# Attention values kept undivided, their divisors sent through DRAM to the output projection

## The chip, the core and the metric

The kernel runs on one core of one Trainium2 chip. A core has five engines with an instruction queue each: PE (matmuls), DVE (vector operations), ACT (activations and copies), POOL and SP (here only the issuing of DMAs). Sixteen DMA engines move data between DRAM and the core's memory, SBUF; matmul results stand in a small memory of their own, PSUM. The metric is device time in microseconds (us) for one execution of the whole program; "before" is 4280.88 us, the median of three runs (4253.56 to 4290.66).

## What is computed

One inference step of a two-layer decoder (D_MODEL 1024) for two groups at once: 1024 prompt positions and 8 sequences of 8 sample positions. Layer 0 mixes with an RWKV-7 recurrence, layer 1 with attention over 256 keys that an indexer selects; each is followed by a feed-forward network (FFN). The part that the change touches is layer 1's prompt attention and its output projection:

```python
def sparse_attend(q, kg, vg, valid):
    ...
    s = jnp.einsum('bthgd,btshd->bthgs', qg, kg.astype(F32)) * ATT_HEAD_DIM ** -0.5
    s = jnp.where(valid[:, :, None, None, :], s, -jnp.inf)
    p = jax.nn.softmax(s, axis=-1)
    o = jnp.einsum('bthgs,btshd->bthgd', p, vg.astype(F32))
    return o.reshape(B, T, Q_W).astype(q.dtype)
...
            o = attn_fn(j, q, k, v, qi, ki, wi) @ P['att_w_o'][j]
...
        x = x + g_a * o
        h = rms_norm(x, P['norm_g'][i, 1]) * (1 + sc_f) + sh_f
        u = jax.nn.relu(h @ P['w_up'][i])
        x = x + g_f * ((u * u) @ P['w_down'][i])
```

There are 16 query heads of 64 values, 4 to each of 4 key heads. The division by the softmax's sum is linear in each head's output, so it can be made at any point before the projection sums over heads.

## The kernel before

The work is split into two groups: A holds the 64 sample positions and prompt positions 0 to 511 (576 columns), B prompt positions 512 to 1023 (512 columns). Activations stand transposed, features on partitions and positions along the free axis, in eight chunks of 128 features. Matmuls in full precision are made of three: a high part `hi` and a rest `lo` of the activation against a high part `wh` and a rest `wl` of the weight (`mm3`, L140). `loadw` brings 128x1024 weights in (L120, SP), ACT casts the high part (L122), DVE or POOL makes the rest (L126). `split` does the same for activations: ACT the `hi` (L144), DVE the `lo` (L145).

The prompt attention runs tile by tile, 128 positions at a time, four tiles in each group. `att_post` (before it) normalizes and rotates queries and keys and computes the indexer's scores `sc` (L1164, L1166), `topk` finds each row's threshold on DVE (L1204). In `att_tile`, `scores(h)` makes one head's exponentials `sm` and their sums and takes the inverse `rs` (L1277), and `values(h)` takes two heads: it transposes `sm` on PE (`pt`, L1293), copies it (`PT`, L1295), multiplies with the values into one half of a PSUM tile `po` (L1299), and spreads the two inverses over 64 partitions with two more matmuls against the identity into `po`'s other half (L1304). After every second call, for the four heads of one key head, ACT copies the inverses out (`orb`, L1308), DVE multiplies (`oT`, L1310), and a DMA stores the tile to a DRAM buffer, `OA` or `OB` (L1311).

`out_proj` starts with eight loads `yl` from that buffer (L445, one for each chunk of 128 features, that is two heads), splits each into `hi` and `lo`, and then makes eight output chunks; each starts with the first chunk's `hi` and needs all eight. `resid` adds the result to the residual stream on DVE (L397). The FFN follows: `up` (matmuls, ACT's `z` at L416 and L417, `split` into `uh` and `ul`) and `down`. The `yl` tiles come from a pool that also serves the FFN's temporaries: 9 buffers, in the last output projection a pool of 6.

The code is written as generators: A's output projection and FFN are a side stream that advances while B's attention is written, and a list scheduler that goes by estimated durations then puts every engine's instructions in one fixed order, in which they run. So A's FFN matmuls stand between B's attention matmuls on PE, and an instruction that waits holds all that stands behind it on its engine. SP issues nearly every DMA of the program in one order as well. A's `out_proj` is entered at about 2990 us, while B's first tiles are in `att_post`; B's is entered at about 3642 us, when its last tile is done, with some of A's FFN still ahead of it on PE.

Of the kernel before, what the change touches and what calls it, by code (L numbers as in the profile page):

```python
# [15 lines left out]
ALU = mybir.AluOpType  # L16
# [3 lines left out]
D = 1024  # L20
# [57 lines left out]
class Kern:  # L78
# [357 lines left out]
            self.fbs = fb  # L436
            yield "fb"

    def out_proj(self, g, l, W_, src, x):

        nc, W = self.nc, g.W
        hi, lo = self.new_hl()
        for k in range(8):
            t = self.tmp("yl")
            nc.sync.dma_start(t[:, 0:W], src[k, :, 0:W])  # L445
            self.split(t[:, 0:W], self.ch(hi, k, W), self.ch(lo, k, W))
        xs = [(self.ch(hi, k, W), self.ch(lo, k, W)) for k in range(8)]
        for m in range(8):
            h, lw = self.loadw(W_[:, m * 128:m * 128 + 128].rearrange("(k p) f -> p k f", p=128), 128, 1024)
            self.mm3(g, [(h[:, k * 128:k * 128 + 128], lw[:, k * 128:k * 128 + 128]) for k in range(8)], xs, self.resid(g, l, 2, x, m))  # L450
            yield
# [791 lines left out]
    def att_tile(self, g, i, pp, bias, Lm):  # L1243


        nc = self.nc
        c0, n, kind, r0 = g.tiles[i]
        j = r0 // 128
        L = r0 + 128
        T1 = lambda nm, shape, dt=F32, tag=None, bufs=None: pp.tile(shape, dt, name=nm, tag=tag or nm, bufs=bufs)  # L1250
        nb = (L + 511) // 512
        nsm, npt, nq = (4, 3, 1) if Lm > 512 else (3, 2, 1)
        q = {}
        sms = {}
        out = {}

        def scores(h):
            gk, hh = divmod(h, 4)
            if hh == 0:
                qn = T1("qnl", [128, 4, 2, 64], bufs=nq)  # L1260
                for b in range(2):
                    nc.sync.dma_start(qn[:, :, b, :], self.scr["P" + g.name][i, :, gk * 256:gk * 256 + 256].rearrange("t (h d) -> t h d", d=64))
                q[gk] = self.att_q(pp, lambda h: qn[:, h].rearrange("p b d -> p (b d)"))
            qh, ql = q[gk]
            sm = T1("sm", [128, Lm], bufs=nsm)
            st = T1("st", [128, 4], bufs=6)
            mn, sums, rs = st[:, 0:2], st[:, 2:3], st[:, 3:4]
            for b in range(nb):
                k0, kn = b * 512, min(512, L - b * 512)
                ps = self.pss.tile([128, 512], F32, name="sp", tag="s")  # L1270
                self.att_qk(ps[:, 0:kn], qh, ql, hh, gk, k0, kn)
                nc.vector.tensor_tensor_reduce(out=sm[:, k0:k0 + kn], in0=ps[:, 0:kn], in1=bias[:, k0:k0 + kn], scale=-0.125, scalar=3.0e38,
                                               op0=ALU.add, op1=ALU.min, accum_out=mn[:, b:b + 1])
            if nb > 1:
                nc.vector.tensor_tensor(out=mn[:, 0:1], in0=mn[:, 0:1], in1=mn[:, 1:2], op=ALU.min)  # L1275
            nc.scalar.activation(out=sm[:, 0:L], in_=sm[:, 0:L], func=AF.Exp, scale=-1.0, bias=mn[:, 0:1], accum_out=sums)  # L1276
            nc.vector.reciprocal(out=rs, in_=sums)  # L1277
            sms[h] = sm, rs

        def values(h):  # L1280

            gk, hh = divmod(h, 4)
            if hh == 0:
                out[gk] = self.psy.tile([128, 512], F32, name="po", tag="y")
            pr = slice(hh // 2 * 128, hh // 2 * 128 + 128)
            half = lambda p: slice(p * 64, p * 64 + 64)
            for j0 in range(0, j + 1, 4):
                jn = min(4, j + 1 - j0)
                PTs = []
                for p in range(2):  # L1290
                    ps = self.lps("pt")
                    for jj in range(jn):
                        nc.tensor.transpose(ps[:, jj * 128:jj * 128 + 128], sms[h + p][0][:, (j0 + jj) * 128:(j0 + jj) * 128 + 128], self.ident)  # L1293
                    PT = T1("PT", [128, 512], bufs=npt)
                    (nc.scalar.copy if p else nc.vector.tensor_copy)(PT[:, 0:jn * 128], ps[:, 0:jn * 128])  # L1295
                    PTs.append(PT)
                for jj in range(jn):
                    for p in range(2):
                        nc.tensor.matmul(out[gk][half(p), pr], self.V[:, j0 + jj, gk * 64:gk * 64 + 64], PTs[p][:, jj * 128:jj * 128 + 128],  # L1299
                                         start=(j0 + jj == 0), stop=(j0 + jj == j))  # L1300

            for p in range(2):
                rs = sms.pop(h + p)[1]
                nc.tensor.matmul(out[gk][half(p), 256 + hh // 2 * 128:384 + hh // 2 * 128], rs.to_broadcast([128, 64]), self.ident, start=True, stop=True)  # L1304
            if hh == 2:
                po = out.pop(gk)
                rb = T1("orb", [128, 256])
                nc.scalar.copy(rb, po[:, 256:512])  # L1308
                oT = T1("oT", [128, 2, 128], bufs=2)
                nc.vector.tensor_tensor(out=oT, in0=po[:, 0:256].rearrange("p (a t) -> p a t", a=2), in1=rb.rearrange("p (a t) -> p a t", a=2), op=ALU.mult)  # L1310
                nc.sync.dma_start(self.scr["O" + g.name][gk * 2:gk * 2 + 2, :, c0:c0 + 128].rearrange("k p t -> p k t"), oT)  # L1311

        scores(0)
        scores(1)
        for h in range(0, 16, 2):
            if h < 14:
                scores(h + 2)
                scores(h + 3)
            values(h)
            yield  # L1320

    side = iter(())
    due = 0.0
# [21 lines left out]

    def att_prompt(self, g):
        self.scratch("O" + g.name, [8, 128, 576])
        with ExitStack() as ctx:
            P = lambda n, b, c=ctx, **k: c.enter_context(self.tc.tile_pool(name=n, bufs=b, **k))
            scp = P("asc", 1)  # L1350
            tk = P("atk", 1)
            S = [scp.tile([128, 640 + 128 * i], F32, name="sc%d" % i) for i in range(4)]
            with ExitStack() as c2:
                pp = P("attg", 1, c2)
                self.psl = P("psl4", 4, c2, space=PSUM)
                post = [self.att_post(g, i, pp, S[i]) for i in range(4)]
                self.together(RATES["post0B"], post[0:2])
                self.together(RATES["post2B"], post[2:4], [self.topk(tk, S[0:2])])
            pp = P("attt", 1)
            self.pss = P("pss", 2, space=PSUM)  # L1360
            self.psl = P("psl1", 1, space=PSUM)
            self.psy = P("psy", 1, space=PSUM)
            tiles = [self.att_tile(g, i, pp, S[i], 1024) for i in range(4)]
            self.together(RATES["tile0B"], tiles[0:2], [self.topk(tk, S[2:4])])
            self.together(RATES["tile2B"], tiles[2:4])

    def att_mixed(self):

        nc, I, g = self.nc, self.I, GA
        LS = PAST + 8  # L1370
        self.scratch("OA", [8, 128, 576])
        with ExitStack() as ctx:
            P = lambda n, b, c=ctx, **k: c.enter_context(self.tc.tile_pool(name=n, bufs=b, **k))
            pp = self.ap2 = P("atts", 1)
# [175 lines left out]
    def run(self):  # L1550
# [42 lines left out]
        self.ada_fin(0, 1)  # L1593
        self.ada_fin(1, 0)
        self.ada_fin(1, 1)
        def mixer(g, l, w, src, x):
            self.mark("out_proj" + g.name)
            yield from self.out_proj(g, l, w, src, x)
            self.mark("ffn" + g.name)
            yield from self.ffn(g, l, x)  # L1600

# [21 lines left out]

        def second(g):
            x = self.reload_x(g)
            yield from mixer(g, 1, self.I["att_w_o"][0], self.scr["O" + g.name], x)
            self.mark("store_y" + g.name)
            self.store_y(g, x)

# [15 lines left out]
        with ExitStack() as ctx:  # L1645
            self.mark("out_projB")
            x = self.xtile("xr", ctx.enter_context(self.tc.tile_pool(name="xp2", bufs=4)))
            old = self.act, self.up_
            self.act, self.up_ = [ctx.enter_context(self.tc.tile_pool(name=n, bufs=b)) for n, b in (("act3", 8), ("up3", 6))]
            x = self.reload_x(GB, x)  # L1650
            run(self.out_proj(GB, 1, self.I["att_w_o"][0], self.scr["OB"], x))
            hl = self.norm_hl(GB, 1, 1, x)
            self.act, self.up_ = old
            self.mark("ffnA")
            run(self.side)
            self.mark("ffnB")
            run(self.ffn(GB, 1, x, hl=hl))
            self.mark("store_yB")
            self.store_y(GB, x)
# [86 lines left out]
```

## Time and profile before

| | |
|---|---|
| time, median of 3 runs | 4280.88 us (4253.56 to 4290.66) |
| the profiled execution: time, span | 4286.67 us, 4284.8 us |
| mean granted TensorE clock | 0.915 |
| busy: PE, DVE, ACT, POOL | 3983.1, 2277.6, 1688.9, 964.0 us |
| A's attention tiles (two halves) | 2172 to 2330, 2330 to 2430 us |
| A's output projection entered | 2990 us |
| B's attention tiles (two halves) | 3272 to 3460, 3460 to 3640 us |
| B's output projection entered | 3642 us |

How to read the rows of the trace: the timeline gives start, duration, engine, line, operation, and output<-inputs, with the idle time of the engine ahead of the instruction and what ended it in brackets; equal neighbours are merged (x8). Line numbers are those of the kernel before. "SPq" is the queue from which DMAs are issued; the duration there is that of issuing, not of the transfer. A window's row gives its length, then for PE, weight loads, DVE, ACT and POOL the busy time and (instructions), then the granted clock as a share of full speed, the mean busy share of the 16 DMA engines and GB/s. A DMA view of a window counts packets, the pieces of a transfer, with their sizes.

### The profile page before, as it was taken

What the parts mean: (1) busy time and instruction counts of PE and PEld (TensorE: products, weight loads), DVE (VectorE), ACT (ScalarE), POOL (GpSimd) and SP (SyncE); (2) the same over time, 40 slices, a digit from 0 to 9 for tenths busy, and PEclk for the clock granted to TensorE, in tenths of its full rate; (3) what the DMA queues carried; (4) which work ended last, traced back from release to release, by engine and by line L of the source; (5) the groups of instructions that cost most, each with busy time, mean ns of one, the idle gap of its engine ahead of it and who ended that gap; (6) DMA issues with size and microseconds to landing.
All of it is one profiled execution on the core that took longest, in us unless ns stands there. A gap on an engine that the chain in (4) does not pass through costs nothing.

```text
span 4284.8 us, 76620 instructions
## 1 busy us (share of the span) xinstructions
PE 3983.1 (93%) x31120; PEld 3196.4 (75%) x31120; DVE 2277.6 (53%) x5534; ACT 1688.9 (39%) x3147; POOL 964.0 (22%) x762
## 2 busy tenths in 40 slices
PE   7998899998999999989799888989988999999999
PEld 5787665666777799989655555778767777988777
DVE  5512775543667533341886954332899854444232
ACT  5632554433445333331454333332443334324332
POOL 1321321311433222212111122222101000222222
PEclk6798787978999999999799999998879999999999
DMA  6676122323322122234332156335211111323332
GB/s 217 203 235 210 51 71 71 95 56 99 111 60 61 46 76 81 83 111 123 118 95 65 50 177 209 120 122 152 91 41 46 45 40 45 118 89 96 94 94 84
DMA packets 555889, 433.84 MB, mean 101 GB/s; under 512 B 93777, under 2 KB 517313, under 8 KB 550354
## 3 DMA queue, kind: packets, MB, share of 16 engines
q1 hardware_dynamic: 549650, 391.20, 30.5%
q0 software_dynamic: 5888, 37.75, 2.5%
q8 instruction: 245, 4.01, 0.4%
q14 instruction: 106, 0.87, 0.1%
HBM read 360.48 MB, written 67.87 MB: 100 GB/s over the span
## 4 chain that ended last, share of the span: by engine, by line
PE 70%; DVE 14%; issue 6%; ACT 3%; DMA 3%; POOL 1%; SPq 0%; DVEq 0%; ACTq 0%; POOLq 0%
PE o L140 42%; DVE tj L1204 3%; PE o L1035 3%; PE po L1299 2%; PE pt L1293 2%; PE sp L1186 1%; PE gp L706 1%; PE tp L733 1%; DMA kvraw<-in_cache_k,ix 1%; PE sp L1185 1%; PE rb L659 1%; POOL wl L126 1%; PE sps L1509 1%; PE tp L754 1%; PE spn L930 1%
## 5 line engine op out<-in xcount | busy, mean ns | idle before, releaser
L126 POOL TENSOR_TENSOR wl<-w,wh 128x1024 fp32r<-128x1024 f32 (+1 forms) x258 | 612.0, 2373 | 2317.3 <-ACT wh L122 2038.6
L140 PE MATMUL o<-hi,wh 128*128 128x512 f32 (+4 forms) x2592 | 882.5, 345 | 21.9 <-ACT hi L144 21.8
L140 PE MATMUL o<-lo,wh 128*128 128x256 f32 (+4 forms) x2592 | 885.9, 343 | 16.4 <-DVE lo L145 11.9
L140 PE MATMUL o<-hi,wl 128*128 128x512 f32 (+4 forms) x2592 | 880.2, 340 | 0.1
L122 ACT CAST wh<-w 128x1024 fp32r<-128x1024 f32 (+3 forms) x388 | 401.3, 1034 | 998.6 <-PE o L140 906.1
L140 PEld LDWEIGHTS o<-hi,wh 128*128 128x128 f32 (+1 forms) x2592 | 498.2, 194 | 75.1 <-ACT hi L144 25.6
L140 PEld LDWEIGHTS o<-lo,wh 128*128 128x128 f32 (+1 forms) x2592 | 499.9, 193 | 70.1 <-DVE lo L145 16.3
L140 PEld LDWEIGHTS o<-hi,wl 128*128 128x128 f32 (+1 forms) x2592 | 498.6, 192 | 48.9 <-issue 11.1
L140 PE MATMUL o<-ul,wh 128*128 128x320 f32 (+2 forms) x1536 | 515.2, 336 | 20.8 <-DVE ul L145 20.7
L140 PE MATMUL o<-uh,wh 128*128 128x320 f32 (+2 forms) x1536 | 511.8, 336 | 2.1 <-DVE tno L1214 1.2
L140 PE MATMUL o<-uh,wl 128*128 128x320 f32 (+2 forms) x1536 | 512.6, 336 | 0.0
L397 DVE SCALAR_TENSOR_TENSOR xr<-o,mods,xr 128x256 f32<-128x256 f32 (+1 forms) x432 | 246.5, 571 | 320.4 <-PE o L140 319.5
L140 PEld LDWEIGHTS o<-ul,wh 128*128 128x128 f32 x1536 | 295.1, 192 | 51.3 <-DVE ul L145 28.3
L140 PEld LDWEIGHTS o<-uh,wh 128*128 128x128 f32 x1536 | 293.4, 192 | 35.1 <-ACT uh L144 8.1
L140 PEld LDWEIGHTS o<-uh,wl 128*128 128x128 f32 x1536 | 295.3, 192 | 25.0 <-issue 5.1
L145 DVE TENSOR_TENSOR ul<-z,uh 128x512 fp32r<-128x512 f32 (+1 forms) x128 | 129.7, 1014 | 319.0 <-ACT uh L144 318.9
L126 DVE TENSOR_TENSOR wl<-w,wh 128x1024 fp32r<-128x1024 f32 (+2 forms) x130 | 161.0, 1238 | 225.2 <-ACT wh L122 223.2
L1035 PE MATMUL o<-wl,hi 128*128 128x256 f32 (+2 forms) x648 | 188.0, 292 | 6.9 <-POOL wl L126 6.9
L1035 PE MATMUL o<-wh,hi 128*128 128x256 f32 (+2 forms) x648 | 187.1, 291 | 6.9 <-ACT hi L144 6.9
L1035 PE MATMUL o<-wh,lo 128*128 128x256 f32 (+2 forms) x648 | 183.9, 291 | 0.0
L1204 DVE TENSOR_SCALAR_CACHE_REDUCE tj<-sc,tcf 128x384 bf16<-128x384 f32 (+2 forms) x192 | 180.7, 941 | 2.8
L1276 ACT ACTIVATE sm<-sm,st 128x128 f32<-128x128 f32 (+7 forms) x128 | 99.3, 775 | 126.6 <-DVE st L1275 79.9
(415 smaller groups left out, 6838.7 us busy)
## 6 DMA issues: line engine op xcount, KB each, us to landing
w<-in_w_up SPq DMA_DIRECT2D x128, 512.0 KB
w<-in_w_down SPq DMA_DIRECT2D x128, 512.0 KB
wa<-in_w_ada SPq DMA_DIRECT2D x96, 512.0 KB
w<-in_rw_w_rkv SPq DMA_DIRECT2D x48, 512.0 KB
w<-in_att_w_in SPq DMA_DIRECT2D x32, 512.0 KB
RA<-pt SPq DMA_DIRECT2D x48, 288.0 KB
RB<-pt SPq DMA_DIRECT2D x48, 256.0 KB
in<-RA SPq DMA_DIRECT2D x32, 320.0 KB
```

Of the source, the lines that this page charges most:

```text
L122: nc.scalar.copy(h[:kp, :n], w[:kp, :n])
L126: eng.tensor_tensor(out=l[:kp, :n], in0=w[:kp, :n], in1=h[:kp, :n], op=ALU.subtract)
L140: nc.tensor.matmul(o[0:M, 0:c1 - c0], a, b[:, c0:c1], start=(i == 0 and q == 0), stop=(i == n - 1 and q == 2))
L145: (lo_eng or self.nc.vector).tensor_tensor(out=lo, in0=src, in1=hi, op=ALU.subtract)
L397: nc.vector.scalar_tensor_tensor(out=xm[:, p0:c1], in0=o[:, p0 - c0:c1 - c0], scalar=self.mods[l][:, j * 8 + m, 8:9], in1=xm[:, p0:c1], op ...
L659: nc.tensor.matmul(ps[half(h), i * n:i * n + n], y(i)[:, h:h + 1].to_broadcast([n, 64]), self.ident[0:n, 0:n], start=True, stop=True)
L706: nc.tensor.matmul(pvs[h][:, c, :], BK[hp, c].rearrange("p b t -> p (b t)")[:, h * 64:h * 64 + 128], AR[hp, c].rearrange("p b t -> p (b t) ...
L1035: nc.tensor.matmul(o[0:n, 0:cw], a, w, start=(k == 0 and q == 0), stop=(k == 7 and q == 2))
L1204: nc.vector.tensor_scalar(out=junk[:, 0:L], in0=s, scalar1=th if isinstance(th, float) else th[:, i:i + 1], scalar2=None, op0=op, op1=ALU. ...
L1276: nc.scalar.activation(out=sm[:, 0:L], in_=sm[:, 0:L], func=AF.Exp, scale=-1.0, bias=mn[:, 0:1], accum_out=sums)
L1293: nc.tensor.transpose(ps[:, jj * 128:jj * 128 + 128], sms[h + p][0][:, (j0 + jj) * 128:(j0 + jj) * 128 + 128], self.ident)
L1299: nc.tensor.matmul(out[gk][half(p), pr], self.V[:, j0 + jj, gk * 64:gk * 64 + 64], PTs[p][:, jj * 128:jj * 128 + 128], start=(j0 + jj == 0 ...
```

## The change

The values leave `att_tile` undivided. The sums' inverses of a tile's 16 heads are gathered in one 128x16 tile `rs16`, transposed once at the tile's end, copied and stored to a new DRAM buffer, `DA` or `DB`, as 16 rows of 128 positions. The two spreading matmuls per call, the copy `orb` and the product are gone; in their place ACT copies `po` to `oT`. `out_proj` loads, behind each `yl`, a tile `dn` whose 128 partitions repeat two rows of that buffer 64 times each, multiplies `yl` by it on DVE, and only then splits. The 64 sample columns of group A, whose values were divided already, are left out of the product.

```diff
-    def out_proj(self, g, l, W_, src, x):
+    def out_proj(self, g, l, W_, src, x, den=None):
...
             nc.sync.dma_start(t[:, 0:W], src[k, :, 0:W])
+            if den is not None:
+
+                d = self.tmp("dn")
+                nc.sync.dma_start(d[:, g.ns:W], den[2 * k:2 * k + 2, g.ns:W].unsqueeze(1).to_broadcast([2, 64, W - g.ns]))
+                nc.vector.tensor_tensor(out=t[:, g.ns:W], in0=t[:, g.ns:W], in1=d[:, g.ns:W], op=ALU.mult)
             self.split(t[:, 0:W], self.ch(hi, k, W), self.ch(lo, k, W))
...
+        rs16 = T1("rs16", [128, 16], bufs=2)
...
-            nc.vector.reciprocal(out=rs, in_=sums)
-            sms[h] = sm, rs
+            nc.vector.reciprocal(out=rs16[:, h:h + 1], in_=sums)
+            sms[h] = sm
...
-            for p in range(2):
-                rs = sms.pop(h + p)[1]
-                nc.tensor.matmul(out[gk][half(p), 256 + hh // 2 * 128:384 + hh // 2 * 128], rs.to_broadcast([128, 64]), self.ident, start=True, stop=True)
+            del sms[h], sms[h + 1]
             if hh == 2:
-                po = out.pop(gk)
-                rb = T1("orb", [128, 256])
-                nc.scalar.copy(rb, po[:, 256:512])
                 oT = T1("oT", [128, 2, 128], bufs=2)
-                nc.vector.tensor_tensor(out=oT, in0=po[:, 0:256].rearrange("p (a t) -> p a t", a=2), in1=rb.rearrange("p (a t) -> p a t", a=2), op=ALU.mult)
+                nc.scalar.copy(oT, out.pop(gk)[:, 0:256].rearrange("p (a t) -> p a t", a=2))
                 nc.sync.dma_start(self.scr["O" + g.name][gk * 2:gk * 2 + 2, :, c0:c0 + 128].rearrange("k p t -> p k t"), oT)
...
+        ps = self.lps("rsT")
+        nc.tensor.transpose(ps[0:16, 0:128], rs16, self.ident)
+        rt = T1("rsT", [16, 128])
+        nc.scalar.copy(rt, ps[0:16, 0:128])
+        nc.sync.dma_start(self.scr["D" + g.name][:, c0:c0 + 128], rt)
+        yield
...
-            yield from mixer(g, 1, self.I["att_w_o"][0], self.scr["O" + g.name], x)
+            yield from mixer(g, 1, self.I["att_w_o"][0], self.scr["O" + g.name], x, self.scr["D" + g.name])
...
-            run(self.out_proj(GB, 1, self.I["att_w_o"][0], self.scr["OB"], x))
+            run(self.out_proj(GB, 1, self.I["att_w_o"][0], self.scr["OB"], x, self.scr["DB"]))
```

The scheduler's order moves from A's first tile on; ahead of it every engine's rows are the same. Line numbers of the changed kernel are some lines higher (L1204 before is L1209 after). Three places matter.

SP at A's entry into `out_proj`, before: the eight loads of the values, then the weights `w` and another tile's stores (`out_v_prompt`, `PB`).

```order
L445 DMA yl<-OA 128x576 x8
L1098 DMA out_v_prompt<-pr 128x256
L120 DMA w<-in_att_w_o 128x8x128
L1097 DMA out_k_prompt<-pr 128x256
L1099 DMA out_idx_k_prompt<-pr 128x64
L1100 DMA PB<-pr 128x1024
L120 DMA w<-in_att_w_o 128x8x128 x3
L1069 DMA pr<-PB 128x2120
```

The same place now (nine more rows, yl and dn by turns, stand ahead of these):

```order
L449 DMA dn<-DA 128x1x512
L445 DMA yl<-OA 128x576
L1102 DMA out_k_prompt<-pr 128x256
L1104 DMA out_idx_k_prompt<-pr 128x64
L1105 DMA PB<-pr 128x1024
L449 DMA dn<-DA 128x1x512
L445 DMA yl<-OA 128x576
L449 DMA dn<-DA 128x1x512
L445 DMA yl<-OA 128x576
L449 DMA dn<-DA 128x1x512
L1103 DMA out_v_prompt<-pr 128x256
L120 DMA w<-in_att_w_o 128x8x128 x4
```

A `dn` load stands behind each `yl`, and all four weight loads behind the last of them.

DVE at the same place, before: `lo` is `out_proj`'s, `pr`, `tc`, `ts`, `kS`, `ql` and `sc` (with the number of its buffer) are the indexer's work for B's next tile, `xr` and `rt` the residual sum.

```order
L145 TENSOR_TENSOR lo<-yl,hi 128x576 x3
L1143 TENSOR_TENSOR kS<-kt,kS 64x4x128
L1143 TENSOR_TENSOR kS<-kt,kS 64x128
L145 TENSOR_TENSOR lo<-yl,hi 128x576 x3
L397 SCALAR_TENSOR_TENSOR xr<-o,mods_112,xr 128x256
L401 TENSOR_TENSOR rt<-o,mods_112 128x64
L397 SCALAR_TENSOR_TENSOR xr<-o,mods_112,xr 128x256
L403 TENSOR_TENSOR xr<-xr,rt 128x64
L1180 TENSOR_TENSOR ql<-qt,qh 64x512
L1164 TENSOR_SCALAR sc_33793<-rl,pr 128x512
```

DVE there now:

```order
L450 TENSOR_TENSOR yl<-yl,dn 128x512 x3
L145 TENSOR_TENSOR lo<-yl,hi 128x576
L1148 TENSOR_TENSOR kS<-kt,kS 64x4x128
L1148 TENSOR_TENSOR kS<-kt,kS 64x128
L145 TENSOR_TENSOR lo<-yl,hi 128x576 x2
L450 TENSOR_TENSOR yl<-yl,dn 128x512 x2
L145 TENSOR_TENSOR lo<-yl,hi 128x576
L1185 TENSOR_TENSOR ql<-qt,qh 64x512
L145 TENSOR_TENSOR lo<-yl,hi 128x576
L450 TENSOR_TENSOR yl<-yl,dn 128x512
L1169 TENSOR_SCALAR sc_33723<-rl,pr 128x512
L450 TENSOR_TENSOR yl<-yl,dn 128x512
```

The products stand among the indexer's rows: `kS` behind the fourth, `ql` behind the sixth, the first `sc` behind the seventh and the next one behind the eighth.

ACT at B's entry, before: `hi` is B's, `z` and `uh` are A's FFN, `wh` a weight.

```order
L122 CAST wh<-w 128x1024
L144 CAST hi<-yl 128x512 x4
L416 ACTIVATE z<-o 128x320
L144 CAST hi<-yl 128x512 x2
L122 CAST wh<-w 128x1024
L416 ACTIVATE z<-o 128x256
L144 CAST hi<-yl 128x512
L417 ACTIVATE z<-z 128x576
L144 CAST uh<-z 128x576
```

ACT there now, from the second of the eight casts on:

```order
L144 CAST hi<-yl 128x512
L122 CAST wh<-w 128x1024
L416 ACTIVATE z<-o 128x256
L144 CAST hi<-yl 128x512
L417 ACTIVATE z<-z 128x576
L144 CAST hi<-yl 128x512
L144 CAST uh<-z 128x576
L416 ACTIVATE z<-o 128x320
L144 CAST hi<-yl 128x512
L122 CAST wh<-w 128x1024
L416 ACTIVATE z<-o 128x256
L144 CAST hi<-yl 128x512
```

All eight casts were done within the first FFN block's `z`; now the seventh and eighth stand in the third block.

More of the change, by code (lines that the diff above doesn't have):

```diff
@@ L1266, in scores @@
             st = T1("st", [128, 4], bufs=6)
-            mn, sums, rs = st[:, 0:2], st[:, 2:3], st[:, 3:4]
+            mn, sums = st[:, 0:2], st[:, 2:3]
             for b in range(nb):
@@ L1292, in values @@
                     for jj in range(jn):
-                        nc.tensor.transpose(ps[:, jj * 128:jj * 128 + 128], sms[h + p][0][:, (j0 + jj) * 128:(j0 + jj) * 128 + 128], self.ident)
+                        nc.tensor.transpose(ps[:, jj * 128:jj * 128 + 128], sms[h + p][:, (j0 + jj) * 128:(j0 + jj) * 128 + 128], self.ident)
                     PT = T1("PT", [128, 512], bufs=npt)
@@ L1347, in att_prompt @@
         self.scratch("O" + g.name, [8, 128, 576])
+        self.scratch("D" + g.name, [16, 576])
         with ExitStack() as ctx:
@@ L1371, in att_mixed @@
         self.scratch("OA", [8, 128, 576])
+        self.scratch("DA", [16, 576])
         with ExitStack() as ctx:
@@ L1595, in run, with mixer @@
         self.ada_fin(1, 1)
-        def mixer(g, l, w, src, x):
+        def mixer(g, l, w, src, x, den=None):
             self.mark("out_proj" + g.name)
-            yield from self.out_proj(g, l, w, src, x)
+            yield from self.out_proj(g, l, w, src, x, den)
             self.mark("ffn" + g.name)
```

## The prediction

> **What bounds the kernel now.** I read the page's busy shares and chain first, then busy time by stage around the code that changes, then the timeline at the two places where the new loads stand.
>
> ```profile
> PE 3983.1 (93%) x31120; PEld 3196.4 (75%) x31120; DVE 2277.6 (53%) x5534; ACT 1688.9 (39%) x3147; POOL 964.0 (22%) x762
> PE 70%; DVE 14%; issue 6%; ACT 3%; DMA 3%; POOL 1%; SPq 0%; DVEq 0%; ACTq 0%; POOLq 0%
> ```
>
> PE carries the chain; whatever makes PE wait is paid in full, and whatever shortens PE's queue is a gain only where PE is full. The stages in question, by window (tiles 1 and 2 of group A, tiles 3 and 4, the first and the second pair of group B, and the step behind them):
>
> ```profile
> 2172.00:2330.00 158.00, 154.04 (x742) 85.27 (x742) 112.23 (x389) 76.78 (x198) 20.71 (x17) 0.95 0.27 72
> 2330.00:2430.00 100.00, 91.91 (x526) 63.45 (x526) 91.31 (x178) 39.48 (x80) 14.29 (x6) 0.98 0.19 54
> 3272.00:3460.00 188.00, 179.24 (x1201) 135.73 (x1199) 167.38 (x471) 69.72 (x135) 17.12 (x7) 0.98 0.17 46
> 3460.00:3640.00 180.00, 180.00 (x1291) 135.22 (x1292) 84.99 (x253) 72.59 (x125) 14.29 (x6) 1.00 0.14 38
> 3640.00:3700.00 60.00, 59.65 (x446) 59.12 (x445) 30.03 (x59) 22.31 (x33) 14.48 (x7) 1.00 0.46 148
> ```
>
> After the window's length come PE, weight loads, DVE, ACT, POOL, then clock, DMA share, GB/s. PE is full in both halves of B (180.00 of 180), near full in A's first half, and DVE is the fuller engine in A's second half (91.31 of 100, PE's 91.91 includes modelled ends).
>
> **The removed matmuls.** Each of 64 calls of `values` (8 tiles, 8 pairs of heads) loses two matmuls at L1304. What one call takes is read at its end, against a block of L1299 without them:
>
> ```profile
> 3628.56 0.27 PE L1304 MATMUL po<-c_ident,st 128*64 128x128 f32 x1
> 3628.66 0.27 PE L1299 MATMUL po<-PT,V 128*64 128x128 f32 x1
> 3628.67 0.48 PE L1304 MATMUL po<-c_ident,st 128*64 128x128 f32 x3
> 3629.09 0.66 PE L1293 MATMUL pt<-c_ident,sm 128*128 128x128 f32 x4
> ...
> 3632.32 1.09 PE L1299 MATMUL po<-PT,V 128*64 128x128 f32 x14
> 3633.34 0.44 PE L1293 MATMUL pt<-c_ident,sm 128*128 128x128 f32 x2
> ```
>
> Without L1304 the next block starts 0.20 after the last start of L1299 (3632.32 + 1.09 - 0.27 = 3633.14, next 3633.34). With it, 0.43 (3628.66 to 3629.09): 0.23, and some 0.04 more for the one that stands ahead: 0.25 us a call, 64 x 0.25 = 16. B's 32 calls stand in a full PE: -8. Of A's 32, half stand where DVE is fuller; I take -5 (0 to -8). Each tile gains one transpose L1323, at most 0.27 like its neighbours: 4 in B, +1. Sum -12, bounds -16 and -6.
>
> **The copies.** ACT's copy and DVE's product become one ACT copy.
>
> ```profile
> L1308 ACT COPY orb<-po x32: 352/372/375, 2182.1 to 3637.8; 128x256 f32<-128x256 f32 x32
> L1310 DVE TENSOR_TENSOR oT<-po,orb x32: 392/420/426, 2182.5 to 3638.2; 128x256 f32<-128x256 f32 x32
> ```
>
> ACT has the same 32 copies plus 8 small ones, DVE loses 32 x 0.42 = 13. In A's second half that is 8 x 0.42 = 3 of DVE's 91, which stands in the -5 above; elsewhere PE covers it. No view shows PE waiting for `po`, so its earlier release is taken at nothing. The 8 stores of a 16x128 tile go out beside `oT`'s and are read hundreds of us later (A), or behind a 4-DMA reload (B): nothing.
>
> **The loads of `dn`, the deciding term.** `out_proj` now issues 16 more DMAs on SP's one queue, each between two `yl` loads. Its source pattern is 2 rows, each repeated 64 times, and 128 rows of 2 KB land, 256 KB. How is a transfer spread? Two windows with a single transfer's packets in them, `oT`'s store (256 pieces of 512 B from 128 partitions) and an 8-row store of 32 B a row:
>
> ```profile
> DMA packets 272, 0.13 MB, mean 66 GB/s; under 512 B 16, under 2 KB 272, under 8 KB 272
> OA<-oT SPq DMA_DIRECT2D x1, 128.0 KB
> ...
> DMA packets 16, 0.00 MB, mean 0 GB/s; under 512 B 16, under 2 KB 16, under 8 KB 16
> ssc<-srow SPq DMA_DIRECT2D x1, 0.2 KB
> ...
> DMA packets 487, 0.93 MB, mean 374 GB/s; under 512 B 27, under 2 KB 36, under 8 KB 486
> q1 hardware_dynamic: 486, 0.93, 101.7%
> ```
>
> Data plus closing packets: 256 + 16 for the first, 8 + 8 for the second. So one closing packet per engine used, and 8 rows took 8 engines although each row could have been halved: the cut goes by the pattern's first dimension. A transfer cut alike on both sides, whose source has 2 in that place, would be cut in 2. Every bulk load of this trace has 16 or more on both sides, so unequal sides are not shown; the ends are 16 engines and 2. I take 2, since the 8-row store is the nearest row. The third pair (loads of 2 KB rows, 3644 to 3646.5) gives an engine's rate: 374 / (16 x 1.017) = 23 GB/s. Over 2 engines one `dn` is 131,072 B / 23 = 5.7 us on each; over 16, 0.7. A `yl` adds 0.8 to every engine, so eight pairs come 6.5 us apart instead of 1.5, and all that is queued behind them on those two engines, weights included, waits too.
>
> The Trainium skill, DMA: Bandwidth & Descriptors, sections "Why a DMA increments its semaphore by 16 and not by 1" and "Rules for kernel authors", says that the slowest dimension of more than one on each side decides, that the largest number up to 16 which divides both is used, and that a small leading dimension confines a DMA. By that rule `dn` has 2 engines and the sum below stands; by rows spread evenly it would be 4274. The trace agrees as far as 8 and 128 rows go.
>
> *Group A's entry*, at 2990, in the middle of B's indexer:
>
> ```profile
> 2990.37 3.73 SPq L445 DMA_DIRECT2D yl<-OA  x8
> 2993.28 1.43 ACT L144 CAST hi<-yl 128x576 fp32r<-128x576 f32 x2 [2.25 <-DMA yl<-OA]
> 3006.61 2.10 DVE L145 TENSOR_TENSOR lo<-yl,hi 128x576 fp32r<-128x576 f32 x3
> 3014.68 1.01 DVE L1166 SCALAR_TENSOR_TENSOR sc<-rl,pr,sc 128x512 f32<-128x512 f32 x2 [0.53 <-ACT rl L1162]
> ```
>
> The first `yl` lands at 2993.3. With `dn` behind it: 2993.3 + 5.7 = 2999.0, the eighth 7 x 6.5 = 45.5 later, 3044.5, and 1.8 for the 688 KB of the other tile's stores between them (at 374 GB/s): 3046. Then product, `hi`, `lo` (0.75 + 0.67 + 0.75): 3048.5, where the last `lo` was done at 3006.61 + 2.10 = 3008.7: 40 late. DVE's order (the change, above) puts the indexer's `kS`, `ql` and `sc` behind these products, so the indexer's second `sc` comes at about 3049 instead of 3014.7, 34 late; PE's order has the output projection and the indexer mixed and stands as well. I take +36, with 28 (more indexer work done in the wait) and 45 as ends. On 16 engines the eight products alone, 6 us of DVE, would stay: +5.
>
> *Group B's entry*, at 3642. Here some 60 us of A's FFN lie ahead on PE, but the engines that empty PSUM for it are in order:
>
> ```profile
> 3646.61 0.37 SPq L120 DMA_DIRECT2D w<-in_w_down  x1
> 3647.04 4.38 SPq L445 DMA_DIRECT2D yl<-OB  x6
> 3655.16 0.43 ACT L416 ACTIVATE z<-o 128x320 f32<-128x320 f32 x1
> 3658.62 0.62 ACT L144 CAST hi<-yl 128x512 fp32r<-128x512 f32 x1 [0.15 <-DMA yl<-OB]
> 3659.15 0.68 ACT L417 ACTIVATE z<-z 128x576 f32<-128x576 f32 x1
> 3659.86 0.67 ACT L144 CAST uh<-z 128x576 fp32r<-128x576 f32 x1
> 3676.32 1.05 ACT L122 CAST wh<-w 128x1024 fp32r<-128x1024 f32 x1 [2.37 <-PE o L140]
> 3677.28 0.38 ACT L416 ACTIVATE z<-o 128x256 f32<-128x256 f32 x1
> 3680.52 0.42 PE L140 MATMUL o<-ul,wh 128*128 128x320 f32 x1 [0.28 <-DVE ul L145]
> ```
>
> In the new order the `hi` casts stand between the `z` of three of the four FFN blocks. SP has the `w_down` load (3646.6) ahead of the first `yl`, so: 3647.0 + 2.9 (as at A: 2990.37 to 2993.28) + 5.7 = 3655.6 for the first `dn`, 7 x 6.4 = 44.8 more for the eighth, 2.8 for two weight loads of 512 KB between them: 3703. Then product and `hi` (1.4), and on ACT two blocks' remains, two `wh`, three `z`, two squares, two `uh` (2 x 1.05 + 1.2 + 2 x 0.68 + 2 x 0.67 = 6.0), and DVE's `ul` 0.75: PE gets the fourth block's `ul` at 3711 instead of 3680.5. PE can run only four PSUM tiles ahead of ACT, so it stands: +31, ends 22 and 38.
>
> Sum: -12 + 36 + 31 = +55. The profiled execution took 4286.67, 5.8 above the median 4280.88 of runs from 4253.56 to 4290.66; the terms are added to the median: 4281 + 55 = 4336. The ends give 4281 - 16 + 28 + 22 = 4315 and 4281 - 6 + 45 + 38 = 4358.
>
> **The rivals.**
>
> *The loads spread over 16 engines; faster than before.* Then B's loads hide under the FFN (PE is 59.65 of 60 there) and A's entry costs the products alone: 4281 - 12 + 5 = 4274. For it: nothing here shows unequal sides, and the destination has 128 rows. It decides when a `dn` takes under about 1.5 us (eight pairs then add under 12). Against it: the 8-row store.
>
> *Two engines, but B's entry hides.* If ACT's `z` did not have to wait (the casts' positions cost little, because PSUM's four tiles and weights already loaded bridge it), only A pays: 4281 - 12 + 36 + 3 = 4308. Against it: the order on ACT.
>
> *Two engines, and slower still.* Sixty-four reads of one row may not run at a load's rate; no row shows them. At twice the time a `dn` is 11.4 and each entry grows by 8 x 5.7 = 46: 4336 + 92 = 4428.
>
> **How the numbers follow.** Forecast 0.58, spread loads 0.20, A's entry alone 0.15, twice as slow 0.07. About 1% (43 us: 4238 and 4324) is what a measurement of this kernel tells from no change. The forecast's own range, with some 10 for the runs' scatter, is 4305 to 4368; about 0.72 of it lies above 4324. Slower: 0.58 x 0.72 + 0.07 + 0.02 from A's entry alone = 0.51. Faster by 43 would need more than all that the change removes: 0.03. Same 0.46. For 8 in 10 the range goes down to the spread loads, 4268, and up to 4372; outside are a third of that rival (0.07), the last one (0.07) and the forecast's top.
>
> **What would show it.** L1304 gone, and blocks of L1299 followed 0.20 later by the next. At the two entries: a DMA share near 2/16 for some 45 us, PE idle in most of it, DVE waiting at L450 for a DMA at intervals near 6.5 us. If `dn` lands within 2 us of its `yl`, the forecast's main step is wrong; if PE stays full behind B's tiles, the step on ACT's order is.

## The result, and the profile after

The changed kernel takes 4322.94 us (median of four runs, 4309.17 to 4341.95), the kernel before 4279.41 in the runs beside it (median of four, 4253.56 to 4290.66). The ratio is 1.0111, 95% interval 1.0067 to 1.0156, that is 43.5 us slower, between 29 and 67. The forecast was +55 and 4336, with a range of its own from 4305 to 4368. Of the ten executions of the two-load kernel below, one took 6868.56 us; it stands in that kernel's median and in no ratio.

The page of the changed kernel has less PE work, and loads of `dn` now stand by name in the chain that ended last (second row, by line). This chain was followed back only to 2328 us, so its shares can't be set beside those of the kernel before, whose chain reaches back to 106 us:

```profile
PE 3973.5 (92%) x30872; PEld 3189.0 (73%) x30872; DVE 2285.9 (53%) x5518; ACT 1689.2 (39%) x3155; POOL 966.6 (22%) x762
PE o L140 21%; DVE tj L1209 3%; PE o L1040 2%; PE po L1305 2%; DMA kvraw<-in_cache_k,ix 1%; PE pt L1299 1%; PE sp L1191 1%; DMA dn<-DB 1%; PE sp L1190 1%; PE sps L1518 1%; DMA dn<-DA 1%; DVE ul L145 1%; PE ip L1191 1%; PE ktp L1509 1%; SPq L445 1%
```

PE has 9.6 us less to do (3983.1 before), and the execution is longer all the same: PE waits more. To find where, both traces are cut at the same pieces of work. The rows that carry the cuts, first of the kernel before (the view by tile: duration of one, then first and last start), the value matmuls of the attention tiles, the last of the indexer's products, and the `yl` loads at the two entries:

```profile
L1299 PE MATMUL po<-PT,V x1152: 272/273/476, 2173.7 to 3637.3; 128*64 128x128 f32 x192
L1186 PE MATMUL ip<-kS,ql x80: 218/494/793, 2121.5 to 3179.4; 64*128 64x512 f32 x48, 64*128 64x384 f32 x16, 64*128 64x128 f32 x8, 64*128 64x256 f32 x8
L445 SPq DMA_DIRECT2D yl<-OA x8: 383/427/439, 2990.4 to 2993.7; - x8
L445 SPq DMA_DIRECT2D yl<-OB x8: 320/427/1385, 3642.5 to 3654.8; - x8
```

and of the kernel after:

```profile
L1305 PE MATMUL po<-PT,V x1152: 272/273/324, 2177.2 to 3660.8; 128*64 128x128 f32 x192
L1191 PE MATMUL ip<-kS,ql x80: 219/496/793, 2124.9 to 3206.3; 64*128 64x512 f32 x48, 64*128 64x384 f32 x16, 64*128 64x128 f32 x8, 64*128 64x256 f32 x8
L445 SPq DMA_DIRECT2D yl<-OA x8: 383/4736/5374, 2983.9 to 3017.1; - x8
L445 SPq DMA_DIRECT2D yl<-OB x8: 383/2563/5789, 3669.6 to 3707.6; - x8
```

The stretches between these cuts, and the same for every kernel of the experiments, in us. "A up to its entry" goes from the first value matmul to the first `yl<-OA`; "A's entry" from there to the last of the indexer's products; "B's tiles" to the last value matmul of B (with the old tiles, the last L1304, 0.2 us later); "behind B" to the end of the span:

| kernel | ahead | A up to its entry | A's entry | B's tiles | behind B | sum without "ahead" |
|---|---|---|---|---|---|---|
| before | 2173.7 | 816.7 | 189.0 | 458.1 | 647.3 | 2111.1 |
| before, again | 2157.3 | 817.2 | 189.0 | 457.2 | 647.9 | 2111.3 |
| after | 2177.2 | 806.7 | 222.3 | 454.5 | 679.4 | 2162.9 |
| no division | 2167.2 | 806.6 | 188.8 | 453.7 | 647.7 | 2096.8 |
| two loads | 2158.8 | 803.4 | 187.2 | 452.1 | 652.3 | 2095.0 |
| cut in 4 | 2178.1 | 804.9 | 197.3 | 460.8 | 661.4 | 2124.4 |
| A's entry alone | 2184.5 | 807.0 | 222.0 | 454.7 | 653.9 | 2137.6 |
| before, `yl` cut in 2 | 2184.0 | 815.1 | 215.0 | 457.2 | 678.2 | 2165.5 |
| POOL's queue | 2172.2 | 803.2 | 202.3 | 453.8 | 666.4 | 2125.7 |
| divided on POOL | 2177.9 | 810.1 | 185.8 | 465.1 | 648.0 | 2109.0 |
| A's tiles alone, two loads | 2171.8 | 806.2 | 185.3 | 457.2 | 648.7 | 2097.4 |

After minus before: -10.0, +33.3, -3.6 and +32.1, together +51.8. "Ahead" holds the same instructions in all of them, but for a few of the first tile in the kernel that divides on POOL.

*A's entry.* DVE after, the first four and the eighth product, with the idle time ahead of each and what ended it, and `lo` and `sc` behind the eighth:

```profile
2992.50 0.69 DVE L450 TENSOR_TENSOR yl<-yl,dn 128x512 f32<-128x512 f32 x1 [0.89 <-issue]
2998.73 0.69 DVE L450 TENSOR_TENSOR yl<-yl,dn 128x512 f32<-128x512 f32 x1 [2.87 <-DMA dn<-DA]
3004.87 0.69 DVE L450 TENSOR_TENSOR yl<-yl,dn 128x512 f32<-128x512 f32 x1 [5.46 <-DMA dn<-DA]
3011.30 0.69 DVE L450 TENSOR_TENSOR yl<-yl,dn 128x512 f32<-128x512 f32 x1 [5.73 <-DMA dn<-DA]
...
3037.63 0.69 DVE L450 TENSOR_TENSOR yl<-yl,dn 128x512 f32<-128x512 f32 x1 [5.52 <-DMA dn<-DA]
...
3039.10 0.75 DVE L145 TENSOR_TENSOR lo<-yl,hi 128x576 fp32r<-128x576 f32 x1
3039.77 0.74 DVE L1171 SCALAR_TENSOR_TENSOR sc<-rl,pr,sc 128x512 f32<-128x512 f32 x1
```

The eight products stand 5.9 to 7.8 us apart, 6.4 in the mean, and all but the first wait for their `dn`. What the DMA engines do from 2995 to 3035 (a digit or a number for each of 40 slices), the same with its share for three us without other transfers, and PE in the stalls of A and B:

```profile
DMA  1821111831111389911116611113811114597116
GB/s 51 245 102 48 49 49 51 229 120 51 49 49 49 81 255 335 365 61 51 51 49 116 240 49 53 49 49 74 274 53 47 51 49 146 130 261 225 57 49 139
```

```profile
2999.00:3002.00 3.00, 1.17 (x7) 0.97 (x7) 0.42 (x1) 0.67 (x1) 0.00 (x0) 0.90 0.13 50
2994.00:3038.00 44.00, 20.47 (x74) 16.50 (x74) 11.79 (x22) 8.67 (x19) 0.00 (x0) 0.58 0.37 115
3680.00:3727.00 47.00, 23.70 (x148) 22.37 (x146) 12.07 (x18) 10.26 (x19) 2.39 (x1) 0.76 0.30 98
```

Between the short bursts of other transfers the core moves 49 to 51 GB/s at a share of 0.13: two of 16 engines, at some 25 GB/s each. PE is busy 20.47 of 44 us here, at a granted clock of 0.58.

*B's entry* is the last window above: PE 23.70 of 47 us. ACT after, the first, the third and the last of the eight casts and the fourth FFN block behind them, then one of PE's waits and the DVE row that makes this block's `ul`:

```profile
3681.86 0.62 ACT L144 CAST hi<-yl 128x512 fp32r<-128x512 f32 x1 [7.67 <-DVE yl L450]
3682.39 0.43 ACT L416 ACTIVATE z<-o 128x320 f32<-128x320 f32 x1
...
3695.05 0.62 ACT L144 CAST hi<-yl 128x512 fp32r<-128x512 f32 x1 [5.55 <-DVE yl L450]
3695.58 0.68 ACT L417 ACTIVATE z<-z 128x576 f32<-128x576 f32 x1
...
3726.95 0.62 ACT L144 CAST hi<-yl 128x512 fp32r<-128x512 f32 x1 [4.98 <-DVE yl L450]
...
3732.52 0.67 ACT L144 CAST uh<-z 128x576 fp32r<-128x576 f32 x1
```

```profile
3722.03 0.64 PE L140 MATMUL o<-uh,wh 128*128 128x320 f32 x1 [9.43 <-ACT z L416]
...
3733.23 1.34 DVE L145 TENSOR_TENSOR ul<-z,uh 128x576 fp32r<-128x576 f32 x1 [1.66 <-ACT uh L144]
```

`z` and `uh` belong to A's FFN, whose matmuls PE could run (the row of PE shows it idle for 9.43 us until such a `z`); they stand on ACT behind casts that wait for DVE's products, and those wait for `dn`.

### The profile page after: what moved, and what is told of

It is laid out like the page before. It is cut to its first block, busy times and chain, and to the rows that moved or that the text cites. A ratio compares the mean times of both kernels' runs of the same rounds, so it can differ in the third digit from the quotient of the medians.

```text
span 4340.2 us, 76161 instructions
## 1 busy us (share of the span) xinstructions
PE 3973.5 (92%) x30872; PEld 3189.0 (73%) x30872; DVE 2285.9 (53%) x5518; ACT 1689.2 (39%) x3155; POOL 966.6 (22%) x762
## 5 line engine op out<-in xcount | busy, mean ns | idle before, releaser
L140 PE MATMUL o<-hi,wl 128*128 128x256 f32 (+4 forms) x2592 | 881.0, 341 | 4.8 <-DVE wl L126 3.7
L1209 DVE TENSOR_SCALAR_CACHE_REDUCE tj<-sc,tcf 128x384 bf16<-128x384 f32 (+2 forms) x192 | 180.6, 941 | 2.6
```

The source lines that it names most:

```text
L140: nc.tensor.matmul(o[0:M, 0:c1 - c0], a, b[:, c0:c1], start=(i == 0 and q == 0), stop=(i == n - 1 and q == 2))
L1209: nc.vector.tensor_scalar(out=junk[:, 0:L], in0=s, scalar1=th if isinstance(th, float) else th[:, i:i + 1], scalar2=None, op0=op, op1=ALU. ...
```

## The experiments

The theory: each `dn` load runs on two engines, because its source pattern is 2 by 64 by 512, and this costs some 33 us at each entry; the tiles gain a dozen. Rivals: the repeated reads themselves are slow; the products cost the time; B's loss comes from A's entry, later.

Beside these kernels the kernel before took 4269.14 us (the first four), 4270.03 (the next three) and 4268.99 (the last), some ten less than beside the changed kernel. The expected times count from 4279 to 4281, so they are to be judged by the ratios and the stretches.

**Two loads for each `dn`**, one row repeated 64 times in each:

```diff
-                nc.sync.dma_start(d[:, g.ns:W], den[2 * k:2 * k + 2, g.ns:W].unsqueeze(1).to_broadcast([2, 64, W - g.ns]))
+                for q in range(2):
+                    nc.sync.dma_start(d[q * 64:q * 64 + 64, g.ns:W], den[2 * k + q:2 * k + q + 1, g.ns:W].to_broadcast([64, W - g.ns]))
```

> The changed kernel with each dn load made as two, one for each row, whose source pattern is 64 repeats of one row of 512. The bytes, the repeated reads and the products are the same; only the first dimension of the source is 64 in place of 2. Theory of the cut (a transfer goes over as many engines as divide the first dimension of both sides): 16 engines, dn lands within 1.5 us of its yl, both stalls go; -13 and +5 for the products at A's entry, 4271 us (4262 to 4280). Rival of the repeats (64 reads of one row are slow by themselves, however they are cut): the stalls stay, 4315 to 4335. Rival of the added work (16 loads, 16 products): no change from the changed kernel, 4320 or more, since 16 loads more are issued.

4276.51 us (median of ten) against 4269.14, ratio 1.0028 (0.9988 to 1.0068). A's entry is back at 187.2, the stretch behind B at 652.3. The bytes, the number of bytes per row, the repetition and the products are those of the changed kernel; each load is made as two, whose pattern has 64 in first place instead of 2. What DVE's products waited for, from the view by tile, first after, then with two loads:

```profile
  DMA dn<-DB: 39.0, 8
  DMA dn<-DA: 32.1, 7
```

```profile
  DMA dn<-DB: 11.9, 5
```

At A no idle time of DVE is put down to `dn` any more. At B 11.9 us of waits are left and 4.6 us of time (652.3 against 647.7 without any division, below). The gain of 8 us that was expected is in the stretches (-16.1), not in the times, whose interval goes from -5 to +29.

**The kernel before with its own `yl` loads cut in two**, 2 by 64 rows, with no repetition, no `dn` and no product:

```diff
-            nc.sync.dma_start(t[:, 0:W], src[k, :, 0:W])
+            nc.sync.dma_start(t[:, 0:W], src[k, :, 0:W].rearrange("(b a) n -> a b n", a=2) if l else src[k, :, 0:W])
```

> The kernel before, with the source of the attention's 16 yl loads written as 2 by 64 rows (even rows, then odd rows, so the projection's input features stand in another order than its weights; no row is repeated and nothing is added). Theory of the cut: the loads go over 2 engines, one takes about 288 KB / 2 / 23 = 6.4 us (A) or 5.7 (B), and both entries wait as in the changed kernel: +30 at A, +20 to +30 at B, 4330 to 4345 us. Rival of the repeats: no row is repeated, so 4279 us as before. Rival of the added work: 4279 as well.

4352.06 us (four runs), ratio 1.0212 (1.0134 to 1.0291); the entries take 215.0 and 678.2, that is 26.0 and 30.9 more than before. The issues on SP's queue at A's entry, and the DMA engines from 3007 to 3040:

```profile
2999.07 34.64 SPq L445 DMA_DIRECT2D yl<-OA  x8
```

```profile
DMA  1111111111111111111111111111111111111111
GB/s 50 50 50 50 50 50 50 50 50 50 50 50 50 50 50 50 50 50 50 50 50 50 50 60 50 50 50 50 50 50 50 50 50 50 50 50 50 50 50 56
```

A plain transfer of 128 rows whose first dimension is 2 runs at the same 50 GB/s as the repeated one. So the cut makes the loss, and reading a row 64 times costs nothing beside it.

**Repeats written as 4 by 16** in each of the two loads:

```diff
+                    nc.sync.dma_start(d[q * 64:q * 64 + 64, g.ns:W], den[2 * k + q:2 * k + q + 1, g.ns:W].unsqueeze(0).to_broadcast([4, 16, W - g.ns]))
```

> As the two-load kernel, but the 64 repeats of a row are written as 4 by 16. Theory of the cut: 4 engines, 131072 B / 4 / 23 = 1.4 us a load, two to a chunk, and 0.8 for the yl: chunks come 3.7 us apart, the eighth 26 us after the first; +14 at A's entry, +5 to +10 at B's, -13: 4285 us (4278 to 4295), between the two-load kernel and the changed one. Rival of the repeats: as the two-load kernel, whatever that is. Rival of the added work: as the two-load kernel.

4288.69 us (ten runs), ratio 1.0043 (1.0001 to 1.0086). Its first and its eighth product at A's entry, and the window from 2992 to 2994:

```profile
2990.86 0.68 DVE L451 TENSOR_TENSOR yl<-yl,dn 128x512 f32<-128x512 f32 x1
...
3017.47 0.69 DVE L451 TENSOR_TENSOR yl<-yl,dn 128x512 f32<-128x512 f32 x1 [1.55 <-DMA dn<-DA]
...
2992.00:2994.00 2.00, 1.70 (x6) 1.48 (x7) 2.00 (x7) 0.25 (x1) 0.00 (x0) 0.50 0.26 98
```

The products stand 3.8 apart in the mean, against 6.4, although a pair's two loads carry the same 256 KB; the DMA share is 0.26 and the rate 98 GB/s, twice what they were, as four engines would give. With a first dimension of 2, 4 and 64 A's entry takes 222.3, 197.3 and 187.2, and the stretch behind B 679.4, 661.4 and 652.3: the same bytes, and the time goes by the cut. B's tiles took 460.8 here, 6 to 9 more than in the others with these tiles. In this trace the granted clock fell there: it was 0.89 from 3270.3 to 3360.3, with 499 matmuls, and 0.96 to 0.98, with 532 to 539, in the same stretch of the other five.

**No division**: the `dn` loads and the products left out, so nothing divides the prompt's attention.

> The changed kernel without the dn loads and the products: the prompt attention's output stays undivided, so this leaves out the division by the softmax's sum. It measures the part of the change that removes work: by the prediction's terms -12, by the profile of the changed kernel -13: 4266 us (4258 to 4274). If the attention tiles' order had cost something of its own, 4279 or more.

4257.90 us (ten runs), ratio 0.9998 (0.9960 to 1.0035). This is what the tiles are worth where no load is added: the sum without "ahead" is 14.4 below before's, too little for the ratio to show. The two-load kernel has the same A entry (187.2 against 188.8): the eight products on DVE cost nothing there.

**A's entry as changed, B's with two loads.**

> A's entry with the changed kernel's one dn load a chunk (2 by 64), B's with the two loads of 64 repeats each. By the legs of the traces so far (from the first yl of A to the indexer's last matmul 222 us in the changed kernel, 187 in the two-load kernel; from the last attention matmul of B to the end 679 and 652): the first leg is 220 to 224, the second 650 to 654, and the time is that of the two-load kernel plus 33 to 35. If one entry's wait had been given back at the other (a side stream that fell behind catches up, or less of it is left), the second leg would be shorter than 650 or longer than 660.

4320.91 us (four runs), ratio 1.0101 (1.0046 to 1.0155). A's entry takes 222.0, and the stretch behind B 653.9, as with two loads. Nothing of A's loss comes back later, and none of B's loss comes from A: the entries add up.

**The `dn` loads issued from POOL's queue** (`nc.gpsimd` in place of `nc.sync`), with the pattern of the change.

> The changed kernel with its 16 dn loads issued from POOL's queue in place of SP's; source pattern, bytes and products as in the changed kernel. If a load cut in two always goes over the same two engines, the eight loads still come about 6 us apart and both legs stay near 222 and 679 (only the weights behind them on SP come sooner, perhaps -5 at each). If POOL's queue deals its transfers over changing engines, eight loads go side by side: legs near 189 and 655, the time near that of the two-load kernel, 4270 to 4285. If the wait came from SP, which issued each yl only after 5 us, and not from the engines, the legs also fall, and then the loads land 6 us apart without SP waiting.

4293.01 us (ten runs), ratio 1.0033 (1.0004 to 1.0062); 202.3 and 666.4, between the two expectations. The row that gives the time from issue to landing:

```profile
DMA to landing us min/median/max: 8.2/10.5/16.0
```

A load takes longer than the spacing of 6.4 on SP's queue, but several are under way at once, and products come in groups. From 3003 to 3005 these loads are nearly all that moves (0.24 of 0.25 MB):

```profile
3003.00:3005.00 2.00, 0.00 (x0) 0.00 (x0) 0.00 (x0) 0.00 (x0) 0.00 (x0) 0.56 0.35 123
```

A share of 0.35 is between five and six engines, so the loads of POOL's queue do not all go over the same two. On how many each one ran this trace does not show. POOL also stood 23.5 us in six waits for a product to release a buffer before it could issue the next load.

**The inverse multiplied into the probabilities on POOL**, in the kernel before, with neither spreading matmuls nor `dn`:

```diff
+            nc.gpsimd.tensor_scalar(out=sm[:, 0:L], in0=sm[:, 0:L], scalar1=rs, scalar2=None, op0=ALU.mult)
...
-            for p in range(2):
-                rs = sms.pop(h + p)[1]
-                nc.tensor.matmul(out[gk][half(p), 256 + hh // 2 * 128:384 + hh // 2 * 128], rs.to_broadcast([128, 64]), self.ident, start=True, stop=True)
```

> Another way to save the same matmuls: the probabilities themselves are multiplied by the inverse on POOL (one instruction a head on 128 rows of up to 1024), so no matmul spreads the inverses and no load or product is added to the output projection. POOL is busy 17 of 188 us and 14 of 180 in B's tiles; the new work is at most 64 x 2.4 us there, by the 2.37 us of a 128x1024 difference on POOL, which fits if PE's rows have other work ahead while a head waits for it. If it fits, the legs are those of the kernel without division: 141 for A's first tiles, 189 at A's entry, 454 for B's tiles, 648 behind them, 4258 us. If the transposes wait for POOL, A's tiles (150 before) and B's (458) grow instead, by up to 2 us for each of 64 pairs of heads: 4280 to 4400.

4287.76 us (ten runs), ratio 1.0025 (0.9986 to 1.0065). POOL was little used in the tiles, but its operation is long, and it stands between the exponential and the transpose:

```profile
L1278 POOL TENSOR_SCALAR sm<-sm,st x128: 602/1883/3167, 2175.8 to 3627.1; 128x128 f32<-128x128 f32 x16, 128x256 f32<-128x256 f32 x16, 128x384 f32<-128x384 f32 x16, 128x512 f32<-128x512 f32 x16
```

B's tiles grow to 465.1, 7 above before, while A's stretch shrinks by 6.6. The trace puts no more than 1.9 us of PE's idle time and 5.1 of its weight loads' down to POOL, and DVE is busy longer in B's tiles too (347.8 us against 338.1 without the division), so what takes back the matmuls' gain there is not shown.

**Only A's tiles changed, with two loads; B's tiles and projection as before.**

> Group A as changed, with each dn load written as two (16 engines); group B's tiles and its projection as before (divided in the tile, no dn). Theory (the whole gain is in A's tiles, the whole cost in engines per load): the leg from A's first tile to the end of the sample index is 141.0 instead of 150.0, A's entry leg 187 against 189.0, B's tiles 458 and the end behind them 647 as before: 11 us less than before, ratio 0.997. Rival (B's tiles and entry, with two loads, gave the gain that the two-load kernel shows in its legs, 4.5 + ...): then the sum of the legs is no less than that of the kernel before.

4275.76 us (twelve runs), ratio 1.0013 (0.9981 to 1.0045). The stretches come as expected (806.2, 185.3, 457.2, 648.7), 13.7 below before's in sum; the times show no gain.

**The kernel before, once more.**

> The kernel before, once more, for a second set of its legs (first value matmul to the end: 150.0, 385.9, 280.8, 189.0, 458.1, 647.3). If the legs are what the differences rest on, each repeats within 3 us, and the part ahead of the first value matmul (2173.7) may differ by 10 or more. Rival: the legs scatter by 5 us or more each, and the differences of 9 and 4 us read from them are not to be trusted.

One run, 4270.54 us. Its four stretches are within 0.9 of the first profile's, its part ahead is 16.4 shorter. Between kernels with the same tiles the stretch up to A's entry runs from 803.2 to 807.0, so differences of some 5 us can be read from one trace, smaller ones only where several agree (B's tiles: 452.1 to 454.7 in five traces with the new tiles, leaving out the one with the low clock, 457.2 to 458.1 in four with the old). The stretches do not, however, add up to the measured times everywhere: in three of the nine kernels with a ratio its interval lies above them (two loads: -16 by the stretches, -5 to +29 by the interval; A's tiles alone: -14 against -8 to +19; `yl` cut in two: +54 against +57 to +124). The rest lies most likely in the part ahead, which the change does not touch. In it the granted clock varies. The windows from 300 to 600 us of before and after (clock third from the end):

```profile
300.00:600.00 300.00, 266.49 (x3102) 207.24 (x3102) 161.05 (x461) 133.50 (x300) 80.67 (x104) 0.83 0.41 126
```

```profile
300.00:600.00 300.00, 269.77 (x2807) 207.38 (x2805) 145.51 (x409) 124.22 (x275) 72.14 (x94) 0.72 0.38 116
```

At 0.72 PE gets through some 300 matmuls fewer in the same 300 us (2807 against 3102). All eleven traces fall in two groups: five have 0.72 or 0.73 here and 2177.2 to 2184.5 us ahead, six have 0.81 to 0.85 and 2157.3 to 2173.7. After's profiled execution, the slowest of its four (4341.95), is of the first group, but so are two kernels with the old projection (`yl` cut in 2, divided on POOL). Whether changed kernels get a lower clock there more often, or the medians of four to twelve runs only fell so, stays open.

## Why the prediction was right

- *Two engines for a `dn`*: right. 2 was taken from a neighbouring row (8 rows on 8 engines), and the runs with 2, 4 and 64 in first place show it; cutting `yl` by 2 shows that it holds without repetition and in another kernel. The Trainium skill, DMA: Bandwidth & Descriptors, section "Rules for kernel authors", gives the same: the slowest dimension of more than one decides. The traces agree: a DMA share of 0.13 and 50 GB/s at 2, 0.26 and 98 GB/s at 4.
- *A `dn` of 5.7 us and pairs 6.5 apart*: 6.4 in the mean. The eighth product was to come 55.6 us behind the entry (3046 against 2990.4) and came 53.7 behind it (3037.63 against 2983.9).
- *A's entry +36*: +33.3. The last `lo` ended 55.9 behind the entry instead of 18.3, 37.6 late where 40 was forecast, and the indexer's second `sc` 31.5 late where 34 was.
- *B's entry +31*: +32.1, and by the step on ACT's order. PE was to get the fourth block's `ul` 73.5 behind the last value matmul (3711 against 3637.5); DVE ended it 73.8 behind (3733.23 + 1.34 against 3660.8). The rival in which B's entry hides falls with it; the kernel with the 2 by 64 loads at A's entry alone, 25.5 faster behind B, shows the same.
- *The removed matmuls, -12*: the sum was near (-13.6 in the stretches), its parts were not, and that their errors cancel is luck. (Its 0.23 and 0.04 make 0.27 a call, not 0.25, 17 us on PE instead of 16.) A was put at -5, because DVE was the fuller engine in its second half; it is -10. The last rows of `po` in A's tiles and the window of these tiles, before and after:

```profile
2421.77 0.48 PE L1304 MATMUL po<-c_ident,st 128*64 128x128 f32 x3
2174.00:2404.00 230.00, 219.25 (x1110) 129.60 (x1110) 177.11 (x513) 104.17 (x251) 29.25 (x20) 0.96 0.25 67
```

```profile
2406.86 1.09 PE L1305 MATMUL po<-PT,V 128*64 128x128 f32 x14
2177.00:2407.00 230.00, 218.94 (x1088) 129.76 (x1089) 182.68 (x522) 111.70 (x271) 30.52 (x21) 1.00 0.26 70
```

  The last of them starts 248.3 behind the first before (2421.98 - 2173.7) and 230.4 after (2407.68 - 2177.2): the tiles themselves shrank by 17.9, more than their 32 x 0.25 on PE, and 8 of it were lost again ahead of A's entry; what takes them there was not examined. The windows show what the sum had no term for: the granted clock is 1.00 in these tiles now and was 0.96, and so it is in all seven traces with the new tiles in A against the three with the old ones. An estimate from these numbers, 0.04 of 230 us, makes that worth up to 9 us, about what the removed matmuls leave open. Why the clock differs is not shown. B was put at -7, with PE full, and gave -3.6; in B's first pair of tiles the prediction's own row has PE busy for 179.24 of 188 us and DVE for 167.38. With the old tiles in B and the new ones in A, B's tiles took 457.2. What keeps B's gain small was not tested.
- *Products cost +5 at A if the loads are spread*: wrong in place. They cost nothing at A; products and doubled loads together cost 4.6 behind B. The rival of spread loads came to -7; the two-load kernel has -16 by its stretches and between -5 and +29 by its times.
- *Twice as slow by repetition*: fell. The repeated and the plain transfer both ran at 49 to 50 GB/s.
- *The signs*: L1304 is gone, PE is idle in about half of both windows (23.5 of 44, 23.3 of 47), DVE waits at 5.9 to 7.8. The DMA share was named as near 2/16 for 45 us; the mean was 0.37 and 0.30, since other transfers come in bursts between, and only the quiet stretches between them show the two engines (0.13).

The two profiled executions are 55.3 apart (4341.95 and 4286.67): 51.8 in the stretches, 3.5 ahead of them. The medians are 43.5 apart; the 8 between them and the stretches are within the interval of 29 to 67.

## What to carry to other kernels

Read a DMA's access pattern as the number of engines it will use: two rows repeated 64 times each are one transfer of 128 rows on two engines, and two transfers of 64 rows are on many. Moving the division behind the tiles took 14 us off them here, and its loads, in order on one queue, cost 65; price the place where the load arrives, not only the place where the matmul leaves. Where the gain is 14 us in 4280, cut the trace at the same pieces of work, because the total cannot show it.

## What was not expected of the hardware

- SP itself stands while it issues. Before, an issue of `yl` took 0.43 us (median). SP's queue after, at A's entry:

```profile
2983.93 0.38 SPq L445 DMA_DIRECT2D yl<-OA  x1
...
2986.19 3.20 SPq L445 DMA_DIRECT2D yl<-OA  x1
...
2990.05 5.32 SPq L445 DMA_DIRECT2D yl<-OA  x1
...
3022.83 5.33 SPq L1103 DMA_DIRECT2D out_v_prompt<-pr  x1
3028.25 23.87 SPq L120 DMA_DIRECT2D w<-in_att_w_o  x4
```

  Behind two `dn` the third `yl` took 3.20 us to issue, the fourth 5.32, and `out_v_prompt` behind the last pair 5.33. (The last row is four issues merged, with the waits between them: singly they took 0.37 to 5.02.) With `yl` cut in two, eight issues stand in 34.64 us. So a transfer on two engines also holds up the issue of others behind it on the queue.
- PE's stall goes with a lower clock: 0.58 in A's 44 us, 0.76 in B's 47. The same matmul after in this stall and behind B's entry, where PE is full:

```profile
3013.41 0.47 PE L140 MATMUL o<-hi,wh 128*128 128x320 f32 x1
...
3676.11 0.31 PE L140 MATMUL o<-hi,wh 128*128 128x320 f32 x1
```

- The same instructions in the same order take 2157 to 2185 us in the part ahead, while the stretches behind it in the two profiles of before repeat within 1 us. The stretch where the granted clock was 0.72 or 0.73 in five executions and 0.81 to 0.85 in six is one place where this shows.
